# Late adaLN vectors of a hybrid diffusion layer: weighted sums on ScalarE and GpSimd in place of two-column fp32 matmuls

## The chip, the cores and the metric

One core of a Trainium2 chip runs one layer of the backbone at batch 1, with 256 latent and 256 context tokens of width 2048. The metric is the device time of one execution in microseconds (us). Five engines work at once, each through its own list of instructions and strictly in that list's order: TensorE (PE, with its weight loads PEld), VectorE (DVE), ScalarE (ACT), GpSimd (POOL) and SyncE (SP), which issues nearly all DMAs. Engines wait for one another by semaphores. An instruction that waits holds up everything behind it on its own engine.

## The reference, cut to what matters

```python
mod_x = (silu(c) @ w_mod + b_mod)[:, None, :]      # w_mod (2048, 12288), fp32
mod_c =  silu(c_ctx) @ w_mod + b_mod
sh1x, sc1x, gt1x, sh2x, sc2x, gt2x = split(mod_x, 6)
ux = modulate(rms_norm(x, g0), sh1x, sc1x)          # the same for the context, with mod_c
mx = token_mixers(uc, ux, ...)                      # conv, mLSTM, gated DeltaNet, RWKV-7; gates; w_out
x  = x + gt1x * rms_norm(mx, g1)
fx = conv_ffn(modulate(rms_norm(x, g2), sh2x, sc2x), ffn_up, ffn_dw, ffn_down)
return x + gt2x * rms_norm(fx, g3)
```

One matrix, `w_mod`, gives six vectors of 2048 per stream. The first two (shift and scale of the mixer) are needed at once, for latent and context tokens. The other four are needed late and for the latent stream alone: shift and scale of the FFN, and the two gates, `gt1x` behind the mixer and `gt2x` at the end. The order of the mixer's work matters too: every branch is a recurrence (or a convolution) on columns of one input projection, and all four branches are merged by `w_br`, with sigmoid gates that are themselves 8192 columns of the input projection.

## The kernel before, in words

The large products are split fp32: each weight tile of 256 rows by 512 columns (512 KB, tile `raw`) is loaded by SP, copied to `hi` on ACT (L192), and `lo = raw - hi` is made on DVE (L194); TensorE then runs three passes (`hi*uh`, `hi*ul`, `lo*uh`). One such tile is called a weight step here. Four `raw` buffers and two each of `hi` and `lo` turn over.

The program is, in order of its text: phase 0 (norm, first adaLN vectors, first columns), RWKV columns and scan, the columns of DeltaNet, mLSTM, convolution and output gates, then `gd_scan`, `conv_module`, `ml_scan`, then `gates` (16 blocks of 512 columns of branch gates, 128 weight steps, kept in DRAM as `dg`), then `merge` (for each branch, 4 blocks of `w_br`, times the gates reloaded as tile `sig`, summed in `mg`), `out_proj` (32 weight steps of `w_out`), and `ffn` (176 steps of `ffn_up`, 88 rows of `ffn_down`).

A planner sets the real order on every engine: it walks the program with its own estimate of each instruction's cost and lets later, independent work move ahead where the tile memory permits. So the scans are short dependent instructions, and the weight steps of the branch gates run between them as filler. Tile memory is taken from pools that are opened and closed like a stack; a tile in memory that another used before waits until that one is done with.

The late adaLN vectors are a generator, `mod_feed`, of 128 steps (16 blocks of 512 columns, 8 steps of 256 rows each). `feed()` is called behind every weight step and takes adaLN steps at a `rate`: 0.55 from `ml_columns` on, up to 96 steps; 8 steps at once where `ffn` begins, then 0.25 per weight step to 128. One step in `wmod_steps` (L242) loads 512 KB of `w_mod` into `wraw` (one buffer, pool `wmr`; in the FFN the `raw` ring) and runs four fp32 matmuls of 256 columns against `cst`, which holds silu(c) and silu(c_ctx) in the first two of 32 columns; they use four 32-row quarters of the array, and their result is `psw`. After 8 steps, `psw` is copied to `wrows` (L262), and a product with a selection matrix (`sel4` or `selb`) gives `psf`: feature-major for shift and scale, or spread over all partitions for a gate, to which DVE adds the bias (L272) and POOL multiplies the norm's gain (L273).

POOL otherwise has the small steps of the RWKV triangular inverse, half of the 31-tap convolution (tiles `ctap`, `cacc`, L863 and L864), some products in the scans, and the sum `mg += sig` of the merge (L1330).

## Time and profile before

| what | value |
|---|---|
| runs | 2360.63 us median of 3 (2359.28 to 2361.23) |
| span of the profiled execution | 2358.9 us, 1.7 us under the median of the runs |
| PE busy | 2250.4 us, 95% of the span |
| DVE busy | 1478.0 us, 63% |
| ACT busy | 987.1 us, 42% |
| POOL busy | 500.8 us, 21% |
| mean granted TensorE clock | 0.980 |

A row of a group reads: line, engine, operation, output tile <- input tiles, shapes, xcount | busy us in all, mean ns of one | idle time of the engine just before, and what ended it. In the views by stretch each row is a stretch in us from the start, its length, then for each engine its busy us with the number of instructions, then the granted clock, the DMA engines' busy share and GB/s. In the answers on one tile, three numbers are the least, the median and the largest duration in ns. In rows of waits: who waited, for whom, us in all, times, longest. A row of a timeline has start, duration, engine and line; in brackets the idle time before it. An fp32 matmul is two records in the trace. PE's share is an average: where its row is full, taking work from PE can shorten the time; where PE waits for a scan, it can't.

### The profile page before, as it was taken

To read this page: it belongs to the slowest core of one execution; us is meant where nothing else is said; L and a number is where in the kernel's file an instruction comes from. 1 tells how busy PE (TensorE), PEld (TensorE's weight loads), DVE (VectorE), ACT (ScalarE), POOL (GpSimd) and SP (SyncE) were. 2 spreads that over 40 slices of the span, in tenths; PEclk is the share of its full clock that TensorE was granted. 3 is DMA by queue.
4 is the path that set the end of the run, shared out by engine and by line. 5 is a ranking of instruction groups with operands and counts; after the bars stand their busy time and mean duration, and the time that the engine had idled before them with its cause. 6 is when DMAs were issued, how large, how long until landed. Compare 5 with 4: busy or idle time off the path is not lost.

```text
span 2358.9 us, 42865 instructions
## 1 busy us (share of the span) xinstructions
PE 2250.4 (95%) x16820; PEld 1846.2 (78%) x16820; DVE 1478.0 (63%) x3079; ACT 987.1 (42%) x1491; POOL 500.8 (21%) x849
## 2 busy tenths in 40 slices
PE   6979899999999899999999999989999999999998
PEld 3657677877888666767777777779999999998886
DVE  3357866643555976566556478566777677775554
ACT  4225644433444343233225544444444344444443
POOL 0012563533452995000001034010000000000000
PEclk8989899899999999999999999989999999999999
DMA  9934654454666677677668667567767666666563
GB/s 367 347 113 129 180 166 117 133 169 135 184 180 197 184 239 216 208 238 233 189 206 275 185 223 262 184 224 216 225 210 218 208 182 187 180 199 204 193 195 101
DMA packets 273612, 471.97 MB, mean 200 GB/s; under 512 B 41505, under 2 KB 80673, under 8 KB 272417
## 3 DMA queue, kind: packets, MB, share of 16 engines
q1 hardware_dynamic: 273122, 467.14, 63.6%
q8 instruction: 132, 2.16, 0.4%
q10 hardware_dynamic: 288, 2.10, 0.2%
q14 instruction: 70, 0.57, 0.1%
HBM read 440.33 MB, written 28.84 MB: 199 GB/s over the span
## 4 chain that ended last, share of the span: by engine, by line
PE 80%; DVE 8%; DMA 5%; ACT 2%; POOL 2%; issue 2%; SPq 0%; DVEq 0%; ACTq 0%; POOLq 0%
PE psB L79 35%; PE psA L79 20%; PE psD L79 10%; PE psw L79 4%; DVE lo L194 2%; DMA wraw<-in_w_mod 2%; PE psG L79 1%; DMA raw<-in_w_mix 1%; DVE cacc L858 1%; POOL riU L397 1%; PE pVN L79 1%; PE pKS L79 1%; PE pSn L79 1%; ACT hi L192 1%; PE psf L79 1%
## 5 line engine op out<-in xcount | busy, mean ns | idle before, releaser
L194 DVE TENSOR_TENSOR lo<-raw,hi 128x1024 fp32r<-128x1024 f32 (+2 forms) x485 | 603.6, 1246 | 449.7 <-ACT hi L192 440.2
L192 ACT ACTIVATE hi<-raw 128x1024 fp32r<-128x1024 f32 (+2 forms) x488 | 508.4, 1043 | 845.4 <-PE psB L79 383.7
L79 PE MATMUL psB<-u2h,lo 128*128 128x256 f32 x1408 | 396.7, 283 | 0.0
L79 PE MATMUL psB<-u2l,hi 128*128 128x256 f32 x1408 | 396.5, 283 | 0.2 <-DVE u2l L1354 0.2
L79 PE MATMUL psB<-u2h,hi 128*128 128x256 f32 x1408 | 395.5, 285 | 1.1 <-DVE u2h L1353 1.1
L79 PE MATMUL psA<-lo,uh 128*128 128x512 f32 x832 | 336.3, 405 | 12.6 <-DVE lo L194 12.3
L79 PE MATMUL psA<-hi,ul 128*128 128x512 f32 x832 | 329.8, 397 | 0.0
L79 PE MATMUL psA<-hi,uh 128*128 128x512 f32 x832 | 310.0, 404 | 2.2 <-ACT hi L192 2.2
L79 PE MATMUL psB<-uh,hi 128*128 128x256 f32 (+1 forms) x832 | 281.5, 347 | 24.4 <-ACT hi L192 17.8
L79 PE MATMUL psB<-ul,hi 128*128 128x256 f32 (+2 forms) x832 | 278.9, 340 | 0.0
L79 PEld LDWEIGHTS psB<-u2h,hi 128*128 128x128 f32 x1408 | 267.6, 192 | 10.8 <-issue 9.5
L79 PEld LDWEIGHTS psB<-u2l,hi 128*128 128x128 f32 x1408 | 269.9, 192 | 0.5 <-DVE u2l L1354 0.5
L79 PEld LDWEIGHTS psB<-u2h,lo 128*128 128x128 f32 x1408 | 269.8, 192 | 0.1
L79 PE MATMUL psB<-uh,lo 128*128 128x256 f32 (+2 forms) x832 | 263.1, 342 | 6.8 <-DVE lo L194 6.8
L79 PEld LDWEIGHTS psA<-lo,uh 128*128 128x128 f32 x832 | 156.9, 189 | 63.0 <-DVE lo L194 21.7
L79 PEld LDWEIGHTS psB<-uh,hi 128*128 128x128 f32 x832 | 159.9, 193 | 54.8 <-ACT hi L192 20.7
L79 PEld LDWEIGHTS psA<-hi,uh 128*128 128x128 f32 x832 | 153.5, 189 | 51.5 <-issue 15.0
L79 PEld LDWEIGHTS psA<-hi,ul 128*128 128x128 f32 x832 | 157.0, 189 | 33.6 <-issue 1.0
L79 PEld LDWEIGHTS psB<-uh,lo 128*128 128x128 f32 (+1 forms) x832 | 153.8, 192 | 32.3 <-DVE lo L194 9.6
L79 PEld LDWEIGHTS psB<-ul,hi 128*128 128x128 f32 (+1 forms) x832 | 160.6, 193 | 22.0 <-issue 6.1
L1524 DVE TENSOR_TENSOR lo<-raw,hi 128x1024 fp32r<-128x1024 f32 x88 | 107.6, 1225 | 78.3 <-ACT hi L1523 78.2
L1444 DVE SCALAR_TENSOR_TENSOR facc<-fpad,ffdw,facc 128x256 f32<-128x256 f32 x352 | 152.9, 488 | 0.2
(569 smaller groups left out, 3129.1 us busy)
## 6 DMA issues: line engine op xcount, KB each, us to landing
raw<-in_w_in SPq DMA_DIRECT2D x208, 512.0 KB, 4.5
raw<-in_ffn_up SPq DMA_DIRECT2D x176, 512.0 KB, 3.9
wraw<-in_w_mod SPq DMA_DIRECT2D x160, 512.0 KB, 5.3
raw<-in_ffn_down SPq DMA_DIRECT2D x88, 512.0 KB, 4.6
raw<-in_w_br SPq DMA_DIRECT2D x32, 512.0 KB, 4.8
raw<-in_w_out SPq DMA_DIRECT2D x32, 512.0 KB, 4.7
raw<-in_w_mod SPq DMA_DIRECT2D x32, 512.0 KB, 4.0
raw<-in_w_in SPq DMA_DIRECT2D x48, 256.0 KB, 3.7
```

What stands on the lines that cost most here:

```text
L79: self.nc.tensor.matmul(out, lhsT, rhs, start=start, stop=stop)
L192: nc.scalar.activation(hi[s], raw[s], AF.Copy)
L194: (nc.gpsimd if self.pool_lo >= 0 else nc.vector).tensor_tensor(lo[s], raw[s], hi[s].bitcast(F32), ALU.subtract)
L397: eng.tensor_tensor(U16[:, :, t], U16[:, :, t], m[:, :, t], ALU.add)
L858: nc.vector.scalar_tensor_tensor(a, cpad[:, i, t : t + 256], w(i, t), a, ALU.mult, ALU.add)
L1444: nc.vector.scalar_tensor_tensor(s3(acc), pad[:, dy : dy + 4, dx : dx + 64], tap(t, b), s3(acc), ALU.mult, ALU.add)
L1524: nc.vector.tensor_tensor(f(lo), f(raw), f(hi).bitcast(F32), ALU.subtract)
```

## The change

For the 16 late blocks, `wmod_steps` no longer uses TensorE for the products with `w_mod`. For each of the two 128-row halves of a loaded tile, ACT multiplies in place by the per-partition scalar silu(c) (`wacc` or `wraw` <- `wraw`, `cst`, 128x512), and POOL adds the result to `wacc` (128x512 fp32): 256 ACT instructions and 240 POOL instructions in all. At the end of a block, one product with ones sums over the partitions: for a gate vector `ones` (128x128) against `wacc` (512 columns), for shift and scale four products of a 128-column piece of `wacc` with one column of ones. The copy to `wrows`, `selb` and the products with them are gone for these blocks. The blocks of phase 0 keep their matmuls, as `wmod_feat`.

The pools are laid out anew: `wmr` has two buffers each of `wraw` and `wacc` and is opened behind `rw_scan`, not at the start, and a second `wmr2` in the FFN takes the place of the `raw` ring; `mgw` (tile `sig`) has two buffers, not three, and is opened last of the merge's pools; `G1` is opened behind `gd_scan`; the 8 steps taken at once at the start of the FFN are gone, its 32 steps all go at 0.25.

```diff
-    def wmod_steps(self, cb, dst, raws=None, gain=None):
+    def wmod_steps(self, cb, dst, gain=None):
         nc, A = self.nc, self.A
...
-        for j in range(8):
-            wr = raws or self.wmr
-            raw = self.raw() if wr is None else wr.tile([P, 2, 512], F32, tag="wraw", name="wraw")
-            nc.sync.dma_start(out=raw, in_=w[256 * j : 256 * j + 256, 512 * cb : 512 * cb + 512].rearrange("(k p) c -> p k c", p=P))
-            for k in range(2):
-                for h in range(2):
-                    r = slice(64 * h + 32 * k, 64 * h + 32 * k + 32)
-                    self.mm(ps[r, 0:256], self.cst[:, 2 * j + k, :], raw[:, k, 256 * h : 256 * h + 256], start=(j == 0), stop=(j == 7))
+        acc = self.wmr.tile([P, 512], F32, tag="wacc", name="wacc")
+        for j in range(8):
+            raw = self.wmod_tile(self.wmr, cb, j)
+            for k in range(2):
+                t = raw[:, k] if j or k else acc
+                nc.scalar.activation(t, raw[:, k], AF.Copy, scale=self.cst[:, 2 * j + k, 0:1])
+                if j or k:
+                    nc.gpsimd.tensor_tensor(acc, acc, t, ALU.add)
             if j < 7:
                 yield
-        rows = self.stage("f3", 256, "wrows")
-        nc.scalar.activation(rows, ps[:, 0:256], AF.Copy)
+        ps = (self.evp if self.wap is not None else self.aux)("psf")
         if gain is not None:
...
-            ps = (self.evp if self.wap is not None else self.aux)("psf")
-            for h in range(2):
-                self.mm(ps[:, 256 * h : 256 * h + 256], self.selb[:, h], rows)
+            self.mm(ps, self.ones, acc)
             nc.vector.tensor_tensor(dst, ps, bg[0], ALU.add)
             nc.gpsimd.tensor_tensor(dst, dst, bg[1], ALU.mult)
...
+        else:
+            for i in range(4):
+                self.mm(ps[:, i : i + 1], acc[:, P * i : P * i + P], self.ones[:, 0:1])
+            nc.vector.tensor_tensor(dst[:, :, 0], ps[:, 0:4], self.PC["b_mod"][:, 4 * cb : 4 * cb + 4], ALU.add)
...
     def gd_scan(self):
-        self.G[0] = self.pool("g1p", stack=self.ues).tile([P, D], F32, name="G1")
...
         ges.close()
+        self.G[0] = self.pool("g1p", stack=self.ues).tile([P, D], F32, name="G1")
...
     def ffn(self):
+        self.wmr = self.pool("wmr2", bufs=2)
         self.wap, self.rate, self.modmax = None, 0.25, 128
-        self.feed(96 + 8)
...
     def build(self):
-        self.wmr = self.pool("wmr", bufs=1, stack=ues)
...
         self.rw_scan()
+        self.wmr = self.pool("wmr", bufs=2, stack=ues)
...
-        self.mgw = self.pool("mgw", bufs=3, stack=ues)
-        self.mgp = self.pool("mgp", stack=ues)
-        self.mg = self.mgp.tile([P, 2, D], F32, name="mg")
-        self.hlp = self.pool("hlp", bufs=2, stack=ues)
-        self.resp = self.pool("resp", side="right")
+        self.resp = self.pool("resp", side="right")
+        self.hlp = self.pool("hlp", bufs=2, stack=ues)
+        self.mgp = self.pool("mgp", stack=ues)
+        self.mg = self.mgp.tile([P, 2, D], F32, name="mg")
+        self.mgw = self.pool("mgw", bufs=2, stack=ues)
```

Three places show how the planned order moves. The first is POOL while the convolution runs. Before, its taps (`ctap`, `cacc`) stand by themselves:

```order
L863 TENSOR_SCALAR ctap<-cpad,vec 128x256 x2
L860 TENSOR_SCALAR cacc<-cpad,vec 128x256
L864 TENSOR_TENSOR cacc<-cacc,ctap 128x256 x2
L863 TENSOR_SCALAR ctap<-cpad,vec 128x256 x2
L864 TENSOR_TENSOR cacc<-cacc,ctap 128x256 x2
```

Now an addition for adaLN stands behind every pair of a tap's two instructions:

```order
L283 TENSOR_TENSOR wacc<-wacc,wraw 128x512
L875 TENSOR_TENSOR cacc<-cacc,ctap 128x256
L874 TENSOR_SCALAR ctap<-cpad,vec 128x256
L283 TENSOR_TENSOR wacc<-wacc,wraw 128x512
L874 TENSOR_SCALAR ctap<-cpad,vec 128x256
L875 TENSOR_TENSOR cacc<-cacc,ctap 128x256
L283 TENSOR_TENSOR wacc<-wacc,wraw 128x512
```

Before, the adaLN loads began during the mLSTM columns. Now the first stands behind the 119th `hi` copy on ACT, and in the 67 weight steps up to the 186th `hi` copy 33 adaLN steps stand between 60 pairs of taps.

The second place is SP's queue in the second half of the branch gates. Before, with two weight loads (`raw`) to most loads of `w_mod` (`wraw`):

```order
L254 DMA wraw<-in_w_mod 128x2x512
L188 DMA raw<-in_w_in 128x2x512 x2
L254 DMA wraw<-in_w_mod 128x2x512
L188 DMA raw<-in_w_in 128x2x512
L1310 DMA dg_11512<-sig 128x512 x2
L1096 DMA gV<-dV 128x512
L254 DMA wraw<-in_w_mod 128x2x512
L188 DMA raw<-in_w_in 128x2x512 x2
```

Now, from the 186th to the 250th `hi` copy, about one to one (62 adaLN steps to 64 weight steps):

```order
L244 DMA wraw<-in_w_mod 128x2x512
L186 DMA raw<-in_w_in 128x2x512
L1106 DMA gV<-dV 128x512
L244 DMA wraw<-in_w_mod 128x2x512
L186 DMA raw<-in_w_in 128x2x512
L1105 DMA gKd<-dK 128x512
L244 DMA wraw<-in_w_mod 128x2x512
L186 DMA raw<-in_w_in 128x2x512
```

The third place is PE in the mLSTM scan. Its 8 rounds (4 heads, 2 directions) are each `psr` (a logarithmic decay on all partitions), exponentials on ACT, products on DVE, and seven products `psn`. Before, weight products (`psA`) stand between `psr` and the seven `psn` products of a round (of which the first follows six rows below the last row here), and between rounds:

```order
L79 MATMUL psr<-mlr_11159,mlsel 128x256 x2
L79 LDWEIGHTS idb
L79 MATMUL psr<-mlmask,idb 128x256
L79 MATMUL psA<-lo,uh 128x512
L79 MATMUL psA<-hi,ul 128x512
L79 MATMUL psA<-hi,uh 128x512 x2
L79 MATMUL psA<-lo,uh 128x512
L79 MATMUL psA<-hi,ul 128x512
L79 MATMUL psA<-hi,uh 128x512
L79 MATMUL psA<-lo,uh 128x512
L79 MATMUL psA<-hi,ul 128x512
```

Now rounds 3 to 8 stand one behind the other with no weight product between them:

```order
L79 MATMUL psr<-mlmask,idb 128x256
L79 MATMUL psn<-mv,mA 128x129 x7
L79 MATMUL psr<-mlr_11182,mlsel 128x256 x2
L79 LDWEIGHTS idb
L79 MATMUL psr<-mlmask,idb 128x256
L79 MATMUL psn<-mv,mA 128x129 x2
L79 MATMUL psq_11326<-mqT,mkT 128x256 x2
L79 MATMUL psn<-mv,mA 128x129 x5
L79 MATMUL psq_11327<-mqT,mkT 128x256 x2
L79 MATMUL psr<-mlr_11150,mlsel 128x256 x2
```

At that point all 128 steps of the branch gates and 4 steps of `w_br` are done on PE; before, 14 steps of `w_br` stand ahead of the end of the eighth round. On SP the first four `sig` loads, without which the merge cannot empty its PSUM banks, now stand behind ten loads of `w_br`, before behind six.

More of the change, by code (lines that the diff above doesn't have):

```diff
@@ L124, in constants @@
             nc.vector.tensor_copy(self.sel4[64 * h : 64 * h + 64, h], self.sel2[64 * h : 64 * h + 64])
-        self.selb = cp.tile([P, 2, P], F32, name="selb")
-        nc.vector.tensor_copy(self.selb, self.sel4[:, :, 0:1].to_broadcast([P, 2, P]))
         self.ones = cp.tile([P, P], F32, name="ones")
@@ L239, in mode_a, with wmod_tile, wmod_feat @@
         evac(ps)
-    def wmod_steps(self, cb, dst, raws=None, gain=None):
-        nc, A = self.nc, self.A
-        if raws is not None and cb in (0, 4):
+    def wmod_tile(self, pool, cb, j):
+        raw = pool.tile([P, 2, 512], F32, tag="wraw", name="wraw")
+        w = self.A["w_mod"][0, 256 * j : 256 * j + 256, 512 * cb : 512 * cb + 512]
+        self.nc.sync.dma_start(out=raw, in_=w.rearrange("(k p) c -> p k c", p=P))
+        return raw
+    def wmod_feat(self, cb, dst, raws):
+        nc = self.nc
+        if cb in (0, 4):
             ps = self.mmp.tile([P, 512], F32, tag="mm", name="psw")
         else:
-            ps = (self.evp if self.wap is not None else self.aux)("psw")
-        w = A["w_mod"][0]
+            ps = self.evp("psw")
         for j in range(8):
-            wr = raws or self.wmr
-            raw = self.raw() if wr is None else wr.tile([P, 2, 512], F32, tag="wraw", name="wraw")
-            nc.sync.dma_start(out=raw, in_=w[256 * j : 256 * j + 256, 512 * cb : 512 * cb + 512].rearrange("(k p) c -> p k c", p=P))
+            raw = self.wmod_tile(raws, cb, j)
             for k in range(2):
@@ L258, in wmod_steps @@
                     self.mm(ps[r, 0:256], self.cst[:, 2 * j + k, :], raw[:, k, 256 * h : 256 * h + 256], start=(j == 0), stop=(j == 7))
+        rows = self.stage("f3", 256, "wrows")
+        nc.scalar.activation(rows, ps[:, 0:256], AF.Copy)
+        ps = self.aux("psf")
+        for i in range(2):
+            self.mm(ps[:, 4 * i : 4 * i + 4], rows[:, P * i : P * i + P], self.sel4.rearrange("p h c -> p (h c)"))
+        bm = self.PC["b_mod"][:, 4 * cb : 4 * cb + 4].unsqueeze(2).to_broadcast([P, 4, 2])
+        for h in range(2):
+            nc.vector.tensor_tensor(dst[:, 2 * h : 2 * h + 2], ps[:, 0:8].rearrange("p (i h c) -> p h i c", h=2, c=2)[:, h],
+                                    bm[:, 2 * h : 2 * h + 2], ALU.add)
+    def wmod_steps(self, cb, dst, gain=None):
+        nc, A = self.nc, self.A
+        acc = self.wmr.tile([P, 512], F32, tag="wacc", name="wacc")
[6 more added lines that the diff above has]
+                    nc.gpsimd.tensor_tensor(acc, acc, t, ALU.add)
             if j < 7:
                 yield
-        rows = self.stage("f3", 256, "wrows")
-        nc.scalar.activation(rows, ps[:, 0:256], AF.Copy)
+        ps = (self.evp if self.wap is not None else self.aux)("psf")
         if gain is not None:
@@ L1600, in build @@
         self.out_proj()
-        self.wmr = None
         ues.close()
```

12 lines of the change are left out of this document (removed).

## The prediction

> **What bounds the kernel now.** I read the page's busy time and its chain of waits first, then busy time by stretch, then the tile that goes away. The page:
>
> ```profile
> span 2358.9 us, 42865 instructions
> PE 2250.4 (95%) x16820; PEld 1846.2 (78%) x16820; DVE 1478.0 (63%) x3079; ACT 987.1 (42%) x1491; POOL 500.8 (21%) x849
> PE 80%; DVE 8%; DMA 5%; ACT 2%; POOL 2%; issue 2%; SPq 0%; DVEq 0%; ACTq 0%; POOLq 0%
> PE psB L79 35%; PE psA L79 20%; PE psD L79 10%; PE psw L79 4%; DVE lo L194 2%; DMA wraw<-in_w_mod 2%; PE psG L79 1%; DMA raw<-in_w_mix 1%; DVE cacc L858 1%; POOL riU L397 1%; PE pVN L79 1%; PE pKS L79 1%; PE pSn L79 1%; ACT hi L192 1%; PE psf L79 1%
> ```
>
> TensorE is busy 95% of the span and makes 80% of the chain, so time taken from it counts where nothing else ends last. Where that holds is read by stretch: the mixer's columns, the rest of the columns with the convolution, the branch gates with the scans, `out_proj`'s tail and the FFN's first product (columns: PE, PEld, DVE, ACT, POOL, clock, DMA share, GB/s):
>
> ```profile
> 420.00:768.00 348.00, 343.33 (x3968) 282.15 (x3967) 186.07 (x694) 149.40 (x303) 148.20 (x420) 0.98 0.57 170
> 768.00:1077.00 309.00, 290.52 (x2192) 213.15 (x2191) 219.74 (x511) 116.33 (x153) 154.13 (x146) 0.98 0.72 218
> 1077.00:1354.00 277.00, 274.88 (x1733) 204.42 (x1730) 151.73 (x270) 106.75 (x145) 14.09 (x17) 1.00 0.70 216
> 1470.00:1563.00 93.00, 86.61 (x418) 66.78 (x416) 49.85 (x82) 40.12 (x63) 1.17 (x3) 0.98 0.63 203
> 1563.00:1870.00 307.00, 303.29 (x2531) 289.04 (x2531) 224.22 (x378) 129.77 (x170) 11.44 (x6) 0.98 0.70 217
> ```
>
> PE leaves 5, 18, 2, 6 and 4 us idle. The 18 us lie where the convolution holds DVE and POOL. The same stretches for tile `psw` alone, the late adaLN products (PE, PEld, ACT):
>
> ```profile
> 420.00:768.00 348.00, 19.70 (x216) 4.77 (x216) 1.16 (x3) 0.98 0.57 170
> 768.00:1077.00 309.00, 25.44 (x320) 6.29 (x320) 1.90 (x5) 0.98 0.72 218
> 1077.00:1354.00 277.00, 19.26 (x236) 4.70 (x232) 1.53 (x4) 1.00 0.70 216
> 1470.00:1563.00 93.00, 5.17 (x64) 1.76 (x64) 0.00 (x0) 0.98 0.63 203
> 1563.00:1870.00 307.00, 15.13 (x192) 3.88 (x192) 1.47 (x4) 0.98 0.70 217
> ```
>
> In all 84.7 us of PE. That is the most that the change can take away, 3.6% of the span.
>
> **What is removed.** In the first three stretches PE is nearly full, so I count all of 19.70 + 25.44 + 19.26 = 64.4 us: **-64.4**. The 5.17 us before 1563 lie in `out_proj`'s tail, where 6.4 us of PE are idle anyway behind the residual; I count nothing. The FFN's 15.13 us count in full, less what is added there (below).
>
> **What is added on TensorE.** The final products. Their forerunners:
>
> ```profile
> L79 PE MATMUL psf<-sel,wrows 128*128 128x4 f32 x64 | 9.3, 251 | 2.0 <-ACT wrows L262 2.0
> L79 PE MATMUL psf<-wrows,selb 128*128 128x256 f32 x32 | 9.5, 419 | 1.0 <-ACT wrows L262 1.0
> ```
>
> A record of the first kind takes 9.3 / 64 = 0.145 us of PE. A block of shift or scale had 4 records (2 products) and now has 8; eight such blocks come late: 8 x 4 x 0.145 = 4.6 us, and double where each also waits for a weight load of its length. I take **+7**. A gate has 512 fp32 columns before and after: 0.
>
> **What is added on ACT and POOL.** Neither operation stands in the trace in this form. The nearest rows, of the same size, and the convolution's rows on POOL:
>
> ```profile
> L374 ACT ACTIVATE uh<-tmp 128x512 fp32r<-128x512 f32 x16 | 10.1, 632 | 13.5 <-DVE tmp L373 13.4
> L1330 POOL TENSOR_TENSOR mg<-mg,sig x24: 1280/2205/2349, 1387.5 to 1461.3; 128x512 f32<-128x512 f32 x24
> L863 POOL TENSOR_SCALAR ctap<-cpad,vec x60: 919/1031/2227, 767.7 to 919.1; 128x256 f32<-128x256 f32 x60
> L864 POOL TENSOR_TENSOR cacc<-cacc,ctap x60: 723/792/1715, 771.3 to 920.7; 128x256 f32<-128x256 f32 x60
> ```
>
> 256 scalings at 0.632 are 162 us of ACT, which is idle 58% of the span; they cost nothing as long as `hi` isn't late behind them. The 240 additions cost between 1.28 (the least, alone) and 2.2 us (the median beside DVE): 307 to 530 us, as much again as POOL has now. In the mixer there are 180 of them; at the mean, 1.75 us, 315 us. What POOL's work costs TensorE is bounded by the convolution's stretch and its rows:
>
> ```profile
> 768.00:925.00 157.00, 141.59 (x1171) 104.74 (x1171) 129.44 (x267) 63.45 (x87) 145.38 (x136) 0.97 0.70 211
> L194 DVE TENSOR_TENSOR lo<-raw,hi x72: 1206/1226/2014, 772.3 to 1074.5; 128x1024 fp32r<-128x1024 f32 x72
> L1257 DVE TENSOR_TENSOR dn<-dn,mlem x8: 154/157/1251, 1309.9 to 1404.2; 128x2 f32<-128x2 f32 x8
> ```
>
> There PE loses 15.4 us while POOL is busy 145: 0.106 us for each us of POOL. Most `lo` are not drawn out (median 1226, least 1206), but a `dn` of 157 ns once took 1251, the rest of a POOL addition. By 0.106, 315 us cost 33 us; by the median of `lo`, nothing. I take the half, **+16**, because DVE was busy 82% in that stretch and is busy 55% in the gates (151.73 of 277).
>
> The Trainium skill ("SBUF — State Buffer", Who interferes with whom) says that a DVE instruction with two inputs in SBUF and a GpSimd instruction that reads SBUF shut each other out for the whole instruction. The single long `dn` agrees; the medians of `lo` and of `cacc` (792 against a least of 723) do not show that most wait. By the rule in full the term would be an estimated 53 us in the convolution's stretch alone, and not 16.
>
> **What moves: the mLSTM scan without cover.** By the third place above, rounds 3 to 8 have no weight products between them, since adaLN and the scans now reach the end of the gates later than the weight steps. A round, in the timeline of before (start, duration):
>
> ```profile
> 1341.04 1.13 PE L79 MATMUL psr<-mlr,mlsel 4*128 4x256 f32 x4
> 1342.10 0.28 PE L79 MATMUL psr<-mlmask,idb 128*128 128x256 bf16 x1
> 1343.40 0.64 ACT L1242 ACTIVATE mA<-psr,mle 128x128 f32<-128x128 f32 x2
> 1344.41 0.28 DVE L1248 TENSOR_TENSOR mA<-mA,psq 128x128 f32<-128x128 f32 x1
> 1350.18 1.03 PE L79 MATMUL psq<-mqT,mkT 128*128 128x256 f32 x4
> 1350.38 0.17 ACT L1256 ACTIVATE dn<-psn 128x2 f32<-128x2 f32 x1 [0.80 <-PE psn L79]
> 1351.21 0.61 DVE L1263 SCALAR_TENSOR_TENSOR mlh<-psn,dn,mlh 128x128 f32<-128x128 f32 x2
> 1387.62 1.72 PE L79 MATMUL psn<-mv,mA 128*128 128x129 f32 x14
> ```
>
> `psr` to 1342.38 is 1.34 us, ACT to 1344.04 another 1.66, DVE to 1344.69 0.65, `psn` 1.72, the end 1350.38 to 1351.82 1.44: 6.8 us. PE's own part is 1.13 + 0.28 + 1.72 + 1.03 = 4.2, so 2.6 us idle, six times: 16 us. If a round takes as long as this one did, weight products within (1341.04 to 1351.82, 10.8 us), 6.6 x 6 = 40; if the heads overlap, 0. Behind it the merge's first gates must land, and SP issues them behind the scan's memory:
>
> ```profile
> sig<-dg SPq DMA_DIRECT2D x3, 512.0 KB, 8.1
> wraw<-in_w_mod SPq DMA_DIRECT2D x29, 512.0 KB, 4.3
> SPq L254 <- PE psw L79: 41.6, 28, 3.2
> SPq L188 <- DVE lo L194: 102.4, 38, 6.4
> ```
>
> One landing is 8.1 us, between 0 and 8. I take 16 + 8 = **+24**, bounds 0 and 48. The weight steps that ran there as filler are not lost; they run later with PE full, and are in the stretches' busy time.
>
> **What else moves.** `mgw` has two buffers. A `sig` buffer is held for its landing, DVE's two products and two additions on POOL:
>
> ```profile
> L1329 DVE TENSOR_TENSOR sig<-sig,psA x24: 674/680/686, 1386.7 to 1459.8; 128x512 f32<-128x512 f32 x24
> ```
>
> 8.1 + 2 x 0.68 + 2 x 2.2 = 13.9 us, or 6.95 a block with two buffers, where the merge (1354 to 1470, 16 blocks) takes 7.25. It just fits; with a late landing it doesn't: 0 to 8, taken as **+3**. The 8 steps at the FFN's start go into the FFN's quarter rate: 62 additions, 108 us of POOL beside a full DVE; at 0.03 (a third of the convolution's rate, since POOL is otherwise idle there) 3 us, at 0.106 11; with 1 us for the final products waiting on POOL: -15.1 + 4 = **-11**, bounds -14 and 0.
>
> SP is the queue that can stall. The `wraw` load now waits for POOL's second addition, not for `psw` (3.2 us at the longest, above), and 2 buffers turn over. Raw loads stand behind it in the queue, by the second place above. In the second half of the gates PE has 277 - 19.26 = 258 us for 62 adaLN steps, 4.16 us each. A buffer is held 4.3 (landing) + 0.63 + 2 x 1.28 = 7.5 us, 3.75 a step: it fits, so I count 0 here, and the opposite as a rival.
>
> The sum: -64.4 + 7 + 16 + 24 + 3 - 11 = -25.4, from the profiled span of 2358.9 to 2333.5. The runs' median lies 1.7 us above that span: **2335 us**.
>
> **Rivals.** *The full gain.* If the scan's rounds overlap, the landing is hidden and POOL does not hold DVE, 24 and 16 fall away: 2295 us. For it: `lo`'s median. Against: the rounds stand bare in the planned order, and nothing else is there to run.
>
> *GpSimd sets the pace (slower).* At 2.2 us for an addition, as in the merge, and a landing of 5.3 us, the median of all `wraw` loads:
>
> ```profile
> DMA to landing us min/median/max: 3.5/5.3/11.2
> ```
>
> a buffer is held 5.3 + 0.63 + 4.41 = 10.3 us, 5.17 a step against PE's 4.16. SP then holds back the weight loads, `hi` and PE starve, and 62 steps lose 1.0 us each: 62 us, with 8 us of the contention left in the convolution's stretch: -25.4 - 16 + 62 + 8 = +29, 2389 us. It decides where two buffers' turn passes 8.3 us, which is an addition above 1.7 us at a landing of 4.3. For it: the median of `mg`, taken while DVE worked as it does in the gates; the DMA share of 0.70. Against: `cacc` beside a busier DVE is only a tenth over its least. The Trainium skill's rule above, taken in full, speaks for this case: by it additions would wait out each `lo` of 1.2 us.
>
> *The scans set the end.* RWKV, DeltaNet, convolution and mLSTM follow one another on small instructions; if this chain ends the mixer, weight products taken out only leave PE idle, and the mixer gains nothing: -11 + 3, 2353 us. For it: the scans' filler runs out before the mLSTM's end. Against: the chain of waits is 80% PE, and the scans' tiles in it (`pVN`, `pKS`, `pSn`, `riU`) have 1% each.
>
> That the products do not go away can't be: the instructions are gone from the order.
>
> **How the numbers follow.** The forecast has a chance of 0.48 (its own range 2318 to 2354: contention 0 to 33, scan 16 to 40), the full gain 0.17, the pace of GpSimd 0.22, the scans 0.13. A difference under 0.2%, 4.7 us, can't be told from none. Of the scans' case half is within it, with the forecast's upper tail 0.09; slower is the pace's 0.22 and 0.01 of the tail; faster the remaining 0.68. The range of 2290 to 2390 takes in the full gain and the pace of GpSimd at its price; beyond lie additions at 2.2 us in the FFN too.
>
> **What would show it.** Right: no `psw` behind 420 us; `wacc` additions of 1.3 to 2.2 us, median near 1.75; PE idle of 2 to 3 us in each of six rounds and one gap of about 8 before the first `psA` of the merge; the gates' second half near 265 us. The full gain: the rounds in less than 5 us each. The pace: SP's `wraw` load waiting for POOL's addition by tens of us, PE behind it waiting for `hi` or `raw`. The scans: an unchanged start of the merge and more PE idle before it. The forecast is wrong if additions pass 1.7 us in the gates, or if weight products of the FFN are late behind ACT's scalings, which I counted at nothing: 64 of them at 0.632 are 40 us on an engine that has 177 us free there.

## The result, and the profile after

The changed kernel takes 2415.53 us (median; 2414.49 to 2421.98), the kernel before beside it 2359.95: a ratio of 1.0238, 95% interval 1.0222 to 1.0254. It is 56 us slower where 25 us less was forecast, and outside the range.

The first lines of the page and its chain, after:

```profile
span 2414.3 us, 41638 instructions
PE 2219.2 (92%) x15812; PEld 1856.3 (77%) x15812; DVE 1597.9 (66%) x3070; ACT 1129.7 (47%) x1725; POOL 866.4 (36%) x1089
PE 66%; DVE 14%; DMA 7%; POOL 5%; issue 4%; ACT 4%; SPq 0%; DVEq 0%; POOLq 0%; ACTq 0%
```

Three things are to be seen. TensorE has 1008 instructions fewer, but is busy only 31.2 us less (2250.4 before), where the removed products alone were 84.7. Its idle time has grown from 108.5 to 195.1 us. And DVE, from which no work was to come or go, is busy 120 us longer with nine instructions fewer; its share of the chain has gone from 8% to 14%.

The additions themselves, by group and by duration (least, median, largest, in ns):

```profile
L283 POOL TENSOR_TENSOR wacc<-wacc,wraw 128x512 f32<-128x512 f32 x240 | 361.1, 1505 | 271.7 <-ACT wraw L281 142.5
L283 POOL TENSOR_TENSOR wacc<-wacc,wraw x240: 1259/1298/2482, 750.1 to 1851.2; 128x512 f32<-128x512 f32 x120
```

Half of them run in 1.30 us or less, so most additions are not drawn out; DVE's instructions are. Stretches of after (columns as in the prediction's table): the convolution, the first part of the gates with the scans, the bare mLSTM rounds, the start of the FFN, and the last product:

```profile
749.00:933.00 184.00, 150.40 (x922) 114.16 (x921) 159.85 (x274) 87.22 (x123) 158.72 (x134) 0.93 0.68 206
1041.00:1156.00 115.00, 98.56 (x799) 73.83 (x798) 87.74 (x195) 68.77 (x101) 70.88 (x52) 0.93 0.75 226
1339.00:1417.00 78.00, 58.92 (x238) 47.39 (x238) 33.43 (x81) 20.95 (x52) 5.14 (x5) 0.76 0.22 68
1586.00:1674.00 88.00, 60.69 (x455) 58.53 (x456) 79.52 (x113) 54.66 (x92) 50.50 (x36) 0.84 0.61 192
2142.00:2414.00 272.00, 260.95 (x1152) 211.13 (x1150) 144.90 (x185) 115.19 (x153) 5.02 (x4) 0.99 0.52 172
```

The stretches of before that correspond to the first, second, fourth and last of these (the mLSTM rounds had weight products between them then):

```profile
787.00:968.00 181.00, 166.64 (x1305) 120.18 (x1307) 132.26 (x277) 69.63 (x95) 126.70 (x119) 0.98 0.71 214
1077.00:1187.00 110.00, 109.67 (x863) 81.65 (x860) 57.71 (x109) 32.33 (x40) 3.38 (x3) 1.00 0.67 207
1563.00:1625.00 62.00, 58.28 (x463) 55.23 (x464) 48.96 (x94) 30.26 (x45) 8.50 (x4) 0.92 0.67 213
2095.00:2359.00 264.00, 252.70 (x1150) 210.18 (x1148) 144.72 (x185) 115.04 (x153) 5.02 (x4) 0.98 0.55 178
```

PE is idle 34, 16, 19 and 27 us in the first four of after, and 14, 0 and 4 us in the three that correspond before. Its granted clock falls with each of them, to 0.76. The last stretch has the same work as before, no adaLN in it, and is 8 us longer; that is a matter of its own (below).

What a wait looks like, in the timeline of after (start, duration), at the DeltaNet's triangular inverse and at the norm that starts the FFN:

```profile
1061.46 1.44 POOL L283 TENSOR_TENSOR wacc<-wacc,wraw 128x512 f32<-128x512 f32 x1 [1.26 <-ACT wraw L281]
1061.68 1.36 DVE L407 TENSOR_TENSOR gim<-gib,giU 128x120 f32<-128x120 f32 x1
1063.49 0.26 DVE L407 TENSOR_TENSOR gim<-gib,giU 128x112 f32<-128x112 f32 x1
...
1595.28 2.35 POOL L192 TENSOR_TENSOR lo<-raw,hi 128x1024 fp32r<-128x1024 f32 x1 [2.39 <-ACT hi L190]
1595.36 2.28 DVE L108 TENSOR_TENSOR an1ra<-an1ra,an 128x1 f32<-128x1 f32 x1
1597.58 1.27 POOL L283 TENSOR_TENSOR wacc<-wacc,wraw 128x512 f32<-128x512 f32 x1
1597.68 1.19 DVE L109 SCALAR_TENSOR_TENSOR an1ry<-an1ra,an1ry 128x1 f32<-128x1 f32 x1
```

A product of 128x1 (0.16 us elsewhere) that starts 0.08 us behind a POOL instruction ends 0.01 us behind it. (This POOL instruction is one of the three `lo` that POOL makes in both kernels; the one that follows is an addition, and DVE's next product ends 0.02 us behind it.) The DVE instruction is on record as running for the whole time, so it shows in no list of waits. An instruction of 0.2 us on a chain of dependent ones then costs what a whole addition costs.

### The profile page after: what moved, and what is told of

Read it like the earlier page. It is cut to its first block, busy times and chain, and to the rows that moved or that the text cites. A ratio compares the mean times of both kernels' runs of the same rounds, so it can differ in the third digit from the quotient of the medians.

```text
span 2414.3 us, 41638 instructions
## 1 busy us (share of the span) xinstructions
PE 2219.2 (92%) x15812; PEld 1856.3 (77%) x15812; DVE 1597.9 (66%) x3070; ACT 1129.7 (47%) x1725; POOL 866.4 (36%) x1089
## 4 chain that ended last, share of the span: by engine, by line
PE 66%; DVE 14%; DMA 7%; POOL 5%; issue 4%; ACT 4%; SPq 0%; DVEq 0%; POOLq 0%; ACTq 0%
PE psB L79 32%; PE psA L79 14%; PE psD L79 10%; DVE lo L192 4%; DMA wraw<-in_w_mod 4%; POOL wacc L283 2%; DVE facc L1455 1%; PE psG L79 1%; DMA raw<-in_w_mix 1%; PE psw L79 1%; DVE cacc L869 1%; PE psn L79 1%; DVE gim L407 1%; ACT hi L190 1%; DVE giU L408 1%
## 5 line engine op out<-in xcount | busy, mean ns | idle before, releaser
L192 DVE TENSOR_TENSOR lo<-raw,hi 128x1024 fp32r<-128x1024 f32 (+2 forms) x485 | 645.2, 1332 | 377.9 <-ACT hi L190 349.3
L283 POOL TENSOR_TENSOR wacc<-wacc,wraw 128x512 f32<-128x512 f32 x240 | 361.1, 1505 | 271.7 <-ACT wraw L281 142.5
L79 PE MATMUL psB<-u2h,hi 128*128 128x256 f32 x1408 | 400.3, 287 | 6.9 <-DVE h L1460 5.5
L79 PE MATMUL psB<-u2h,lo 128*128 128x256 f32 x1408 | 400.3, 285 | 6.8 <-DVE lo L192 6.8
L79 PE MATMUL psB<-u2l,hi 128*128 128x256 f32 x1408 | 400.9, 285 | 1.7 <-DVE u2l L1365 1.7
L79 PE MATMUL psA<-lo,uh 128*128 128x512 f32 x832 | 348.7, 420 | 45.4 <-DVE lo L192 45.1
L79 PE MATMUL psA<-hi,ul 128*128 128x512 f32 x832 | 338.3, 407 | 0.0
L79 PE MATMUL psA<-hi,uh 128*128 128x512 f32 x832 | 313.9, 411 | 11.0 <-ACT hi L190 7.5
L79 PE MATMUL psB<-uh,hi 128*128 128x256 f32 (+1 forms) x832 | 281.8, 348 | 18.0 <-ACT hi L190 13.6
L79 PEld LDWEIGHTS psB<-u2h,lo 128*128 128x128 f32 x1408 | 272.9, 194 | 7.7 <-DVE lo L192 7.7
L79 PEld LDWEIGHTS psB<-u2h,hi 128*128 128x128 f32 x1408 | 271.7, 194 | 8.9 <-DVE h L1460 5.9
L79 PE MATMUL psB<-ul,hi 128*128 128x256 f32 (+2 forms) x832 | 278.1, 339 | 0.0
L79 PEld LDWEIGHTS psB<-u2l,hi 128*128 128x128 f32 x1408 | 273.1, 194 | 3.3 <-DVE u2l L1365 2.3
L79 PE MATMUL psB<-uh,lo 128*128 128x256 f32 (+2 forms) x832 | 261.0, 340 | 8.3 <-DVE lo L192 8.3
L79 PEld LDWEIGHTS psA<-lo,uh 128*128 128x128 f32 x832 | 162.5, 195 | 102.7 <-DVE lo L192 65.7
L281 ACT ACTIVATE wraw<-wraw,cst 128x512 f32<-128x512 f32 x240 | 160.6, 714 | 136.4 <-DMA wraw<-in_w_mod 120.7
L79 PEld LDWEIGHTS psA<-hi,uh 128*128 128x128 f32 x832 | 159.4, 195 | 51.7 <-ACT hi L190 9.9
L79 PEld LDWEIGHTS psB<-uh,hi 128*128 128x128 f32 x832 | 160.7, 194 | 43.3 <-ACT hi L190 15.9
L79 PEld LDWEIGHTS psA<-hi,ul 128*128 128x128 f32 x832 | 162.9, 196 | 35.1 <-issue 0.9
L79 PEld LDWEIGHTS psB<-uh,lo 128*128 128x128 f32 (+1 forms) x832 | 153.4, 191 | 30.4 <-DVE lo L192 10.8
L79 PEld LDWEIGHTS psB<-ul,hi 128*128 128x128 f32 (+1 forms) x832 | 159.5, 192 | 20.6 <-issue 4.0
```

Of the source, the lines that this page charges most:

```text
L79: self.nc.tensor.matmul(out, lhsT, rhs, start=start, stop=stop)
L192: (nc.gpsimd if self.pool_lo >= 0 else nc.vector).tensor_tensor(lo[s], raw[s], hi[s].bitcast(F32), ALU.subtract)
L281: nc.scalar.activation(t, raw[:, k], AF.Copy, scale=self.cst[:, 2 * j + k, 0:1])
L283: nc.gpsimd.tensor_tensor(acc, acc, t, ALU.add)
```

## The experiments

Where the time went can be read by halves: up to the FFN's first weight step (the 313th `hi` copy on ACT starts), and from there to the end of the profiled span. Times in us; the ratios are to the kernel before, with their intervals.

| kernel | median | ratio | to the FFN | behind it |
|---|---|---|---|---|
| before | 2360 | 1 | 1563.5 | 795.4 |
| changed | 2415.5 | 1.0238 (1.0222 to 1.0254) | 1586.1 | 828.2 |
| zeros written, not added | 2352.8 | 0.9976 (0.9963 to 0.9989) | 1551.4 | 805.1 |
| no additions | 2335.7 | 0.9899 (0.9885 to 0.9914) | 1527.9 | 805.1 |
| old products, new pools | 2381.5 | 1.0092 (1.0077 to 1.0107) | 1557.6 | 822.4 |
| sums on VectorE | 2426.1 | 1.0278 (1.0263 to 1.0294) | 1613.9 | 809.4 |
| old products, new pools, old FFN | 2371.3 | 1.0043 (1.0030 to 1.0056) | 1565.2 | 800.4 |
| before, 3 FFN blocks on VectorE | 2342.8 | 0.9921 (0.9908 to 0.9934) | 1564.5 | 777.0 |
| the same, gate blocks too | 2343.5 | 0.9928 (0.9915 to 0.9941) | 1560.6 | 777.0 |
| changed, one input in the FFN | 2400.2 | 1.0167 (1.0150 to 1.0185) | 1585.4 | 812.6 |
| before, merge pools reordered | 2394.6 | 1.0142 (1.0129 to 1.0155) | 1591.7 | 800.9 |
| 3 FFN blocks and 4 column blocks | 2351.3 | 0.9955 (0.9939 to 0.9970) | 1573.2 | 777.5 |
| 3 FFN blocks, late start | 2379.8 | 1.0086 (1.0069 to 1.0102) | 1605.6 | 772.2 |

The planner orders each of these programs anew, so parts need not add up, and two sums below don't. The two parts are those of the profiled execution; that of the zeros took 5 us more than the median of its ten runs (2349.8 to 2361.6), those of "old FFN" and "gate blocks too" 4 us less than theirs.

This split has a fault. Where the FFN is laid out as before, eight adaLN steps are taken ahead of its first weight step; elsewhere they come behind it, and so their time changes sides. The end of the last `psA` record, the last product of `out_proj`, is a split that does not depend on it:

| kernel | to the last `psA` | behind it |
|---|---|---|
| before | 1553.4 | 805.5 |
| no additions | 1527.3 | 805.6 |
| zeros written, not added | 1550.8 | 805.7 |
| changed | 1585.5 | 828.8 |
| old products, new pools | 1556.9 | 823.1 |
| old products, new pools, old FFN | 1553.3 | 812.3 |
| before, merge pools reordered | 1579.6 | 813.0 |

### What the additions cost: written zeros, and nothing

```diff
-                    nc.gpsimd.tensor_tensor(acc, acc, t, ALU.add)
+                    for _ in range(3):
+                        nc.gpsimd.memset(t, 0.0)
```

> Each addition on POOL is replaced by three writes of zeros over the half tile that it would have read (128x512; in the changed kernel 128x396 took 0.39 us, so about 1.5 us together, the mean of an addition, 1.505). The sums are left out, POOL's time and the time that a wraw buffer is held stay. Theory 1, POOL's read of two tiles shuts DVE out: the 134 us by which DVE instructions beside the additions are longer than their own kind go away, and the time falls to about 2340 us (FFN 33 us less, gates 28, convolution 20); the mLSTM rounds stay bare (about 40 us). Theory 2, the pace of POOL and the ring of two wraw buffers: nothing changes, about 2415 us. Theory 3, only the bare rounds and the pools: about 2415 us too, and DVE's stretching would go without a gain.

The second takes the two lines away altogether.

> The additions are left out altogether (the sums are not made); loads, ScalarE's scalings and the final products stay. Theory 1 (lock): the same as with the writes of zeros, about 2340 us. Theory 2 (pace, ring): about 2340 us here, and 2415 with the writes of zeros. If both stay near 2415 us, ScalarE, the loads' order or the pools are the cause.

Measured: 2352.8 and 2335.7 us. The lock's theory had about 2340 for both, the two others 2415 for the first. The page of the first, with its writes, and of the second:

```profile
span 2356.5 us, 42032 instructions
PE 2200.2 (93%) x15812; PEld 1840.7 (78%) x15812; DVE 1462.3 (62%) x3070; ACT 1127.3 (48%) x1725; POOL 854.8 (36%) x1569
L284 POOL MEMSET wraw<- x720: 515/526/671, 750.9 to 1731.5; 128x512 f32 x180
```

```profile
span 2333.0 us, 41163 instructions
PE 2184.5 (94%) x15812; PEld 1833.9 (79%) x15812; DVE 1472.0 (63%) x3070; ACT 1134.7 (49%) x1729; POOL 509.3 (22%) x849
```

POOL is as busy with the zeros as with the additions (854.8 and 866.4 us, 3 x 0.526 = 1.58 us for each half), and a `wraw` buffer is held as long, yet 63 us are gone, and DVE's same 3070 instructions take 1462.3 us, not 1597.9. Most of the cost is POOL's reading and not its time. Two DVE instructions with two inputs in both kernels: the triangular inverse's `gim` in the gates, after and with the zeros, and `u2l` at the start of the FFN, after and with the zeros:

```profile
L407 DVE TENSOR_TENSOR gim<-gib,giU x30: 167/230/1364, 1061.7 to 1110.7; 128x120 f32<-128x120 f32 x2, 128x112 f32<-128x112 f32 x2, 128x104 f32<-128x104 f32 x2, 128x96 f32<-128x96 f32 x2
```

```profile
L408 DVE TENSOR_TENSOR gim<-gib,giU x30: 163/216/276, 1034.4 to 1073.8; 128x120 f32<-128x120 f32 x2, 128x112 f32<-128x112 f32 x2, 128x104 f32<-128x104 f32 x2, 128x96 f32<-128x96 f32 x2
```

```profile
L1365 DVE TENSOR_TENSOR u2l<-tst,u2h x16: 410/426/1482, 1611.0 to 1645.0; 128x256 fp32r<-128x256 f32 x16
```

```profile
L1366 DVE TENSOR_TENSOR u2l<-tst,u2h x16: 410/425/427, 1573.4 to 1603.6; 128x256 fp32r<-128x256 f32 x16
```

Beside the zeros the longest of them takes 276 ns and not 1364, and 427 and not 1482. The cast `u2h`, with one input, is drawn out too, after and with the zeros:

```profile
L1364 DVE CAST u2h<-tst x16: 278/385/1381, 1610.7 to 1644.5; 128x256 fp32r<-128x256 f32 x16
```

```profile
L1365 DVE CAST u2h<-tst x16: 274/311/704, 1573.0 to 1603.1; 128x256 fp32r<-128x256 f32 x16
```

Its largest goes from 1381 to 704 ns, and to 295 without additions: for a cast, written zeros are not quite free. The Trainium skill ("SBUF — State Buffer", Who interferes with whom) says that the second of two SBUF inputs of a DVE instruction shares a port with GpSimd's reads, that the one who comes first holds it for the whole instruction, and that a GpSimd instruction that only writes does not contend with such a DVE instruction. For instructions with two inputs, these two runs agree with it.

The new order is a rival here: of the same 3070 DVE instructions, 2540 stand at the same place of the list in both kernels, and the 63 us can hold some of that. But an order alone does not draw out an instruction. Counted one by one against the short ones of their own kind in these traces, the DVE instructions of the changed kernel are 137 us longer where an addition runs beside them, as much as DVE's whole loss against the zeros, 136.

The other 17 us, from zeros to nothing, are POOL's time: they fall in the mixer alone (1551.4 to 1527.9 in the profiled executions, which differ by 23; the FFN keeps 805.1). There SP's `wraw` load does wait for POOL, after:

```profile
SPq L244 <- POOL wacc L283: 102.8, 45, 7.2
```

102.8 us in 1041 to 1339, up to 7.2 at a time, with weight loads behind it; before, the same load waited 41.6 us for `psw`. This is the wait that the forecast's slow rival named. All of POOL's time is worth 17 us, not 62, and what part of it goes through this queue is not shown.

The two pages also show what an idle PE costs. From the kernel with no additions to the changed one, PE idle grows by 46.6 us (148.5 to 195.1), and PE busy by 34.7 (2184.5 to 2219.2) with the same 15812 instructions. The second goes with a slower clock behind the gaps: the mean granted clock is 0.971 without additions and 0.959 after.

### How much must POOL read

```diff
-                    nc.gpsimd.tensor_tensor(acc, acc, t, ALU.add)
+                    if self.wap is None:
+                        nc.gpsimd.tensor_scalar(t, t, 1.0, None, ALU.mult)
+                    else:
+                        nc.gpsimd.tensor_tensor(acc, acc, t, ALU.add)
```

> The changed kernel, with the planned order of the mixer unchanged; in the FFN alone each addition on POOL is replaced by a product of one tile with 1 (one input in SBUF, 128x512; the sums of the last gate are left out). Theory 1 in the form 'POOL reading any SBUF tile shuts out DVE': DVE is stretched as with the additions, the FFN keeps its 828 us, about 2415 us or a little more, as the product may take longer than 1.3 us. If it takes two tiles read at once: the FFN falls to about 805 us as with the writes of zeros, about 2392 us.

Measured: 2400.2 us, the FFN 812.6. The product with one input takes longer than an addition, and DVE in the FFN is in between (stretches from the FFN's first step to the end: after, one input, zeros; PE, PEld, DVE, ACT, POOL):

```profile
L284 POOL TENSOR_SCALAR wraw<-wraw x60: 1486/1534/3032, 1596.9 to 1757.8; 128x512 f32<-128x512 f32 x60
1585.00:2398.00 813.00, 773.59 (x5352) 719.61 (x5352) 564.68 (x862) 382.68 (x515) 124.10 (x74) 0.98 0.62 193
```

```profile
1586.00:2414.00 828.00, 779.17 (x5352) 724.46 (x5352) 596.90 (x861) 383.23 (x515) 110.58 (x74) 0.97 0.61 190
```

```profile
1551.00:2356.00 805.00, 770.50 (x5352) 717.06 (x5352) 549.00 (x862) 382.21 (x515) 112.04 (x194) 0.98 0.60 195
```

Over the zeros' 549.0 us, DVE is drawn out by 47.9 us beside 60 additions (0.80 each) and by 15.7 beside 60 products of one input (0.26 each). Neither of the two expectations holds: in the FFN a third of the loss stays with one input, most of it needs two. Why a third, these runs don't tell.

### What the pools cost

The changed kernel's pools with the two-column products of before:

> The changed kernel's pools and order of opening, but with the two-column products of before on TensorE (three wraw buffers, which fill the place of two wraw and two wacc). Only the pools and the FFN's even rate differ from the kernel before. Theory 1: the time of before, 2360 us, plus what the bare mLSTM rounds cost (two rounds here by the planned order) and FFN 5 us: about 2380 us. Theory 3, the pools are the main loss: 2400 us or more.

2381.5 us: up to the FFN's first weight step no longer than before (1557.6), and 27 us more behind it; by the last `psA`, 3.5 us more ahead of it and 17.6 behind. So the FFN's layout was put back:

```diff
-        raw = pool.tile([P, 2, 512], F32, tag="wraw", name="wraw")
+        raw = self.raw() if pool is None else pool.tile([P, 2, 512], F32, tag="wraw", name="wraw")
...
-        self.wmr = self.pool("wmr2", bufs=2)
+        self.wmr = None
...
+        self.feed(96 + 8)
```

> The run before this with the old products in the new pools (2381 us) lost nothing up to the FFN's first weight step and 27 us behind it. Here its FFN is laid out as before: no second pool of wraw buffers, the weight ring instead, and the 8 adaLN steps taken at once. Theory A, the loss of the new layout is the FFN's own: 2381 - 27 + 5 = about 2359 us, with the last product's matmuls back at their pace of before (227 ns from start to start, not 234). Theory B, the mixer's bare mLSTM rounds are the loss: about 2380 us still.

2371.3 us, not 2359. Of the loss, 10 us came back (behind the last `psA`, 823.1 to 812.3). They are the gap at the FFN's start: the 8 steps taken at once had filled it, and without them PE stands idle there. From the FFN's first step on PE is idle 801 - 786.56 = 14.4 us with the old FFN, and 822 - 793.05 = 29.0 with the new one:

```profile
1565.00:2366.00 801.00, 786.56 (x5552) 722.53 (x5552) 534.67 (x819) 342.04 (x437) 17.89 (x11) 0.99 0.62 193
```

```profile
1558.00:2380.00 822.00, 793.05 (x5616) 725.51 (x5616) 545.96 (x861) 346.33 (x453) 19.94 (x14) 0.98 0.60 190
```

What did not come back is the pace of the last product, which the expectation had laid to the FFN's pools. So the merge pools' order alone was put into the kernel before:

```diff
-        self.mgw = self.pool("mgw", bufs=3, stack=ues)
-        self.mgp = self.pool("mgp", stack=ues)
-        self.mg = self.mgp.tile([P, 2, D], F32, name="mg")
-        self.hlp = self.pool("hlp", bufs=2, stack=ues)
         self.resp = self.pool("resp", side="right")
+        self.hlp = self.pool("hlp", bufs=2, stack=ues)
+        self.mgp = self.pool("mgp", stack=ues)
+        self.mg = self.mgp.tile([P, 2, D], F32, name="mg")
+        self.mgw = self.pool("mgw", bufs=2, stack=ues)
```

> The kernel before with one edit: the four pools of the merge are opened in the changed kernel's order (resp, hlp, mgp, mgw, and mgw with two buffers). Products, wmr and FFN are those of before. It is to tell two small terms: where the last product's slower pace comes from (234 ns from matmul to matmul in every kernel with the new pools, 227 in those with the old, the FFN's own pools making no difference), and what the bare mLSTM rounds cost by themselves (rounds 6 to 8 by the planned order). If both are this order's doing: 8 us for the pace, 5 to 10 for the rounds, 2368 to 2378 us. If neither: 2360 us.

2394.6 us: 34 more, twice what was expected at most. SP's queue in that kernel, 1340 to 1420, and the stretch of the bare rounds:

```profile
SPq L1321 <- PE psho L84: 31.4, 1, 31.4
```

```profile
1355.00:1416.00 61.00, 40.78 (x161) 31.30 (x161) 27.36 (x62) 16.53 (x36) 2.08 (x2) 0.72 0.34 112
```

The first `sig` load (L1321) waits 31.4 us, until the mLSTM scan's output has been transposed (`psho`). That fits a `mgw` that, opened last, lies where the scan's tiles lay. Until it lands no `w_br` product can be emptied, the weight products stop at four, and three rounds stand bare, PE 20 us idle at a clock of 0.72. Seven more microseconds are the last product (800.9 behind the FFN's first step, against 795.4; 271.2 against 264.2 from the 488th `hi` copy on, the last of `ffn_up`). Its matmuls, before, with the merge order alone, and after:

```profile
L79 PE MATMUL psD<-hi,hh x352: 387/389/628, 2107.4 to 2348.7; 128*128 128x512 f32 x176
```

```profile
L79 PE MATMUL psD<-hi,hh x352: 392/394/628, 2134.1 to 2382.3; 128*128 128x512 f32 x176
```

```profile
L79 PE MATMUL psD<-hi,hh x352: 392/397/628, 2154.6 to 2403.9; 128*128 128x512 f32 x176
```

By the medians 5 and 8 ns each, 1056 times, at a clock of 0.98 to 0.99. The edit touched the four pools alone, so it comes with their layout, perhaps with where `resp` and what lies behind it are put in memory. That, and why an address should matter, is not shown.

Here the parts do not add up. The merge order alone costs 34 us and the FFN's even rate 10, but all new pools with the old products cost 21. The 23 us that the mixer regains with `wmr` opened later and wider are open. One run asked whether the later start of the adaLN steps is what regains them:

```diff
-        self.rate = 0.55
         self.ml_columns()
+        self.rate = 0.85
         self.conv_columns()
```

> The fastest kernel so far (2343 us), with the late adaLN steps begun behind the mLSTM columns, not with them, and taken at 0.85 for each weight step, not 0.55. This asks why the new pools with the old products lost nothing in the mixer (2381 us, all of it behind the mixer) although their merge order alone cost 34 us: with them the adaLN loads began later, in the convolution's stretch. If the later start is worth those 25 to 30 us by itself: about 2315 to 2320 us. If not: 2343 us or more.

2379.8 us. The edit did more than was meant: at 0.85 the count of steps due ran past 104, and all 24 steps of the last three blocks were taken at once in front of the FFN, where TensorE waited for DVE (`PE psf L79 <- DVE wacc L261`, 36.9 us). Only what lies ahead of it can be used: the 301st `hi` copy starts at 1514.4 us, and at 1516.2 in the same kernel without the edit. This later start gains 2 us. It is not as late as that of the new pools, though: the first product of a late block stands at 580 us here, at 483 without the edit, and at 749 with the old products in the new pools. So the 23 us stay open.

### Sums on VectorE

```diff
-                t = raw[:, k] if j or k else acc
-                nc.scalar.activation(t, raw[:, k], AF.Copy, scale=self.cst[:, 2 * j + k, 0:1])
+                c = self.cst[:, 2 * j + k, 0:1]
                 if j or k:
-                    nc.gpsimd.tensor_tensor(acc, acc, t, ALU.add)
+                    nc.vector.scalar_tensor_tensor(acc, raw[:, k], c, acc, ALU.mult, ALU.add)
+                else:
+                    nc.vector.tensor_scalar(acc, raw[:, k], c, None, ALU.mult)
```

> The same sums on VectorE, each half as one instruction acc = raw * c + acc (128x512, about 0.68 us, 256 of them: 174 us); neither ScalarE nor POOL takes part. Theory 1 (lock): no instruction on DVE is drawn out, but DVE has 174 us more; in the planned order all eight mLSTM rounds stand bare. About 2385 us, under the changed kernel. Theory 2 or 3: 2415 us or more, since DVE is the fuller engine and the rounds are as bare as before.

2426.1 us, where the lock's theory had 2385: this time is the one that the other theories named. No addition on POOL, and still slower than the changed kernel: in the planned order all eight mLSTM rounds stand bare, as `1280.00:1444.00` shows, PE 62 us idle at a clock of 0.69:

```profile
1280.00:1444.00 164.00, 101.73 (x416) 74.35 (x415) 81.97 (x194) 33.72 (x79) 14.37 (x17) 0.69 0.25 79
```

The expectation knew of the bare rounds and put too little on them. By its time alone this run does not speak for the lock; the zeros do.

So the sum was moved only where no scan waits for DVE, with the pools of before: the last three blocks, in the FFN, from its 20th weight step on.

> The kernel before, its pools and mixer untouched; only the last three adaLN blocks, in the FFN, are summed on VectorE (acc = raw * c + acc, 128x512, 48 instructions) with one product with ones, and start 20 weight steps into the FFN. Lock theory: no POOL work, 15 us of two-column products gone, three products of 0.59 x 2 us added, DVE has room there (73% busy): 12 us less, about 2348 us. If instead any extra DVE work in the FFN holds up the lo tiles: 2360 us or more.

2342.8 us, 17 less than before (12 expected), and the fastest kernel here but for the one without sums. The FFN's part falls from 795.4 to 777.0:

```profile
1564.00:2341.00 777.00, 761.40 (x5354) 716.72 (x5354) 563.95 (x877) 340.46 (x436) 17.71 (x11) 0.99 0.65 199
L261 DVE SCALAR_TENSOR_TENSOR wacc<-raw,cst,wacc x45: 745/752/754, 1627.5 to 1894.9; 128x512 f32<-128x512 f32 x45
```

DVE has 27 us more to do than before in this stretch (536.66), PE 20 us less (780.98), and PE's idle time is 15.6 us as against 15.0: all of PE's relief reaches the end. Two steps further gained nothing more:

> As the last one, and the four blocks of the first gate vector (32 steps among the branch gates) are summed on VectorE too, in the pools of before, so that the mLSTM rounds keep their weight products in between. If VectorE's room in the gates (55% busy before) holds 44 us more: another 19 us less, about 2330 us. If the scans' small DVE instructions wait behind it: about 2350 us or more.

2343.5 us. In the mixer 20 us of products went, and the median shows nothing of it. The profiled execution, the fastest of the six, has 4 us (1560.6 against 1564.5).

```profile
1074.00:1341.00 267.00, 252.97 (x1517) 195.06 (x1503) 193.08 (x356) 104.84 (x138) 20.37 (x17) 1.00 0.73 224
```

PE is 14 us idle in the gates (2 before), DVE 72% busy (55% before).

> The fastest kernel so far (three FFN blocks summed on VectorE, 2343 us), with the first four blocks of the FFN's shift summed on VectorE too: 32 steps among the mLSTM columns, where VectorE was 52% busy and PE full. About 21 us of two-column products go; four blocks cost 4 x 8 x 0.145 = 5 us in final products. If VectorE's room holds 44 us: about 2328 us. If the RWKV scan or the convolution is held up by it, as the scans were by the gate's sums: 2343 us or more.

2351.3 us, 9 worse than without the column blocks. The columns and the merge starve PE: between the 71st and the 111th `hi` copy it is idle 10 us (none without), its longest waits being those of the RWKV scan's `psS`; it is idle 9.5 us between the 273rd and the 281st, where the mLSTM's end comes late (0.9 without). The share of time that DVE is free does not tell what a scan can bear.

## Why the prediction was wrong

By its own steps, in us:

| step | predicted | measured |
|---|---|---|
| products removed | -64.4, and -15.1 in the FFN | gone as counted, 84.7 with the burst's |
| final products | +7 | +2.5 (`psf` 13.87 to 16.38 of PE) |
| contention of POOL and DVE | +16, bounds 0 and 33 | +63 (additions against zeros) |
| SP's `wraw` load behind POOL | 0; 62 in a rival | +17 (zeros against nothing) |
| bare mLSTM rounds, `mgw` | +24 and +3 | not measured apart; +34 with the merge order alone, 7 of it the last product's pace |
| FFN's burst | 0 | +10 |
| FFN in all | -11 | +23 behind the last `psA` (+33 behind the first weight step) |

**The step that failed is the contention term.** The row that it was taken from was sound (`dn`, 157 ns drawn out to 1251). Three choices were wrong. First, the price for each POOL microsecond came from the convolution's stretch, where much of POOL's work is `ctap`, which reads one tile (60 x 1.03 of 145 us), and by the run with one input that costs a third of an addition. Second, it was halved because DVE is less busy in the gates; but what is drawn out there is a chain of 0.2 us instructions (`gim`, `giU`, the norm), each by up to an addition, and a chain has no free share. Third, medians were read: half the `lo` tiles are not touched, so their median (1225 after) shows nothing, while the sum over DVE is 136 us more than with the zeros. The `dn` was not a single one either: two of the eight took 1.25 us, and each ended 0.01 us behind an addition of POOL. That an idle PE is paid twice was not known. (The 53 us that the prediction sets beside its 16 stand there without their working.)

Where the additions are left out, the prediction's other terms come out nearly right in the mixer, in sum: -64.4 + 7 + 24 + 3 = -30 against -26 measured (1553.4 to 1527.3). The second half of the gates, forecast at 265 us, takes 266 there, from the 186th to the 250th `hi` copy; 279 with the zeros; and 300 in the changed kernel, against 275 before. The FFN is +23 instead of -11, and all of that is the lock (828.8 against 805.7): the 15 us of products that went were used up by the missing burst (10) and the last product's pace (7).

**Two smaller terms were put at nothing.** A `wraw` buffer was to be held 7.5 us; with the landing of 4.5, the scaling of 0.71 and the additions' mean of 1.48 in the gates it is 8.2, next to the 8.3 from which the prediction's own rival lets two buffers fall behind. And that the burst in front of the FFN cost nothing was true, but it was read as worth nothing: its 5.17 us lay in a gap of PE, and without it that gap is bare.

**The slow rival** named GpSimd, and its time (2389) came nearest, but its mechanism has it the other way round, so it is luck that the time came near. It let additions take 2.2 us and the ring fall behind. The additions kept a median of 1.30 us, and DVE paid. The sign it gave, SP waiting tens of us for POOL, is in the trace, within the 17 us of POOL's time. The full gain fell: even without additions it is 2336 us, not 2295. The scans' end fell by its own sign, an unchanged start of the merge: the 250th `hi` copy starts at 1349 us before, at 1336 after and at 1297 without additions.

**The mLSTM term** had its mechanism right: rounds 3 to 8 are bare, one every 8.6 us (the six `psr` start between 1351.52 and 1394.34), where 6.8 was worked out.

```profile
1386.47 1.10 PE L79 MATMUL psr<-mlr,mlsel 4*128 4x256 f32 x4 [0.34 <-DVE mlh L1274]
1389.52 3.35 PE L79 MATMUL psn<-mv,mA 128*128 128x129 f32 x14 [1.74 <-ACT mA L1253]
1394.34 2.04 PE L79 MATMUL psr<-mlr,mlsel 4*128 4x256 f32 x4 [1.47 <-DVE mlh L1272]
1405.39 0.50 PE L79 MATMUL psA<-hi,uh 128*128 128x512 f32 x1 [3.54 <-DVE mg L1338]
```

PE's idle time in the rounds is 15.5 us against 16, and the wait for the merge's first `mg` 3.5 against 8. What was missed is that `psn` takes 3.35 us between such gaps, 1.72 before. That the merge order alone gives 27 us without the last product's pace, the 24 + 3 of the forecast, is luck: there three rounds are bare, not six.

The measured column comes from different kernels: -84.7 + 2.5 + 63 + 17 + 34 + 10 = +42, against 56, and with the 21 us of all new pools in place of 34 and 10 it would be +19. What does add up is the chain from the kernel before over no additions and zeros to the changed one, at the last `psA`. The mixer goes by -26 with all that is not POOL, +23.5 with POOL's time (17 by the medians) and +35 with its reading; behind it, +0, +0 and +23. That is +55 us. What the first link is made of, products gone against bare rounds, pools and order, is only in part taken apart.

## What to carry to other kernels

Work that is moved to GpSimd is not free because GpSimd is idle: beside each of its two-input instructions here, a DVE instruction lasted up to as long as that one did, and this hurt most where DVE ran short dependent steps; look at the sum of DVE's busy time, not at medians or at waits. Before moving a sum off TensorE, find a stretch where no scan waits for the engine that gets it: 24 steps in the FFN on VectorE gained 17 us, where all 128 on two idle engines lost 56. And a pool's place in the stack is part of the schedule: the merge's four pools opened in another order, its gates' buffers last and two, not three, cost 34 us by themselves.

## What was not expected of the hardware

**An idle TensorE also comes back slow.** In the rounds, with gaps of 1.5 to 1.8 us between groups of matmuls, a `psn` record has a median of 422 ns, 275 before:

```profile
L79 PE MATMUL psn<-mv,mA x112: 271/422/554, 1330.7 to 1401.4; 128*128 128x129 f32 x112
```

```profile
L79 PE MATMUL psn<-mv,mA x112: 271/275/378, 1307.4 to 1403.0; 128*128 128x129 f32 x112
```

The Trainium skill ("TensorE: Matmul & The Clock Gate", Part 1) tells of a clock that is halved until the array has been busy for some 3.4 us. That the `psA` behind the gap at 1405 are at 0.40 us only from 1409.4 on, 4.0 us later, is near it; but here gaps well under 3.4 us, one after the other, are enough to keep it low (0.76 in that stretch).

```profile
1408.55 0.63 PE L79 MATMUL psA<-hi,ul 128*128 128x512 f32 x1
1409.37 0.40 PE L79 MATMUL psA<-lo,uh 128*128 128x512 f32 x1
```

Over the whole kernel, from no additions to the changed one, 35 us of longer matmuls go with 47 us of idle time.

**POOL loses little.** The additions' mean is 1505 ns against a median of 1298: 50 us over 240 of them, where DVE loses 136.

**Matmuls of the last product** take 389 ns with the old layout of the merge's pools, 394 with that layout alone changed and 397 with all the new pools, at nearly the same clock (0.98 to 0.99); why is open.
